# A quarter of the next norm's input, turned by DMA instead of on TensorE

## The chip, the cores and the metric

The kernel runs on one core of one Trainium2 chip. The metric is the device time of one launch in microseconds, as a median over runs.

## The reference

The reference is a two-layer encoder trunk on an input x of 512 tokens by 1024 channels in float32. Each layer adds three branches to x, each behind an RMS norm with a gain per channel, and a last norm ends it:

```python
for l in range(DEPTH):                     # DEPTH = 2
    x = x + 0.5 * swiglu(rms_norm(x, ffn1_norm[l]), ffn1_w_in[l], ffn1_w_out[l])
    x = x + mixer(rms_norm(x, mix_norm[l]), ...)
    x = x + 0.5 * swiglu(rms_norm(x, ffn2_norm[l]), ffn2_w_in[l], ffn2_w_out[l])
return rms_norm(x, final_norm)

def swiglu(x, w_in, w_out):                # w_in 1024 x 5632, w_out 2816 x 1024
    g, u = jnp.split(x @ w_in, 2, axis=-1)
    return (jax.nn.silu(g) * u) @ w_out
```

The mixer joins a neighbourhood attention of eight heads and a two-dimensional Fourier transform per channel group by two gates. Only its beginning matters here: it multiplies its norm's input by a wide matrix, just as an FFN does.

## The kernel before

**Layout and arithmetic.** x lies in SBUF as `x[128, 4, 1024]`: four blocks of 128 tokens, with the tokens on the partitions. A product over channels needs its input the other way round, channels on the partitions, so for each norm x is turned. Every float32 operand of a product is split in two: a high part, rounded by ScalarE (`S.activation(hi, src, AF.Copy)` into float32r), and a low part, the rest, subtracted by VectorE. Three matmuls (high·high, high·low, low·high) make one product. Large products are done by Strassen's scheme with seven products m = 1 to 7 of quarters.

**Weights.** They come in granules of 128 × 1024 (512 KB) in a fixed order, the list of `stage_items`. `Raw.load` asks for one by a DMA on SP's queue. Where the scheme needs the sum of two granules, some sums are made by VectorE (`Item.summed`, L172), others by a second, accumulating DMA from GpSimd's queue (`Raw.summed`, L158), which waits for the first load. `Item.prep` splits a granule (ScalarE L199 or L194, VectorE L202 or L195) into `whi` and `wlo`, which have three buffers each. `Stream.next` hands the next granule to a product after having split up to two more behind it (`AHEAD = 2`); `Stream.prep(to)` splits up to a given place in the list; `fetch` keeps the loads eight granules (`FETCH = 8`) ahead of the splits. `ws` is the stream.

**Order.** Each engine and each queue works in order. The framework lays out the order of every engine when the program is built: instructions that were traced earlier go first, but one whose inputs it believes late is passed by those behind it. Inside `tc.manual_schedule` the engines named keep the written order. `tc.issue_after(ins)` puts instructions of the same engine or queue behind `ins`, without a wait for its end.

**The end of an FFN** (`stage_ffn`, the loop over `steps`). The output product has 21 steps of (m, c), c being one of three chunks of the inner width: (1, 0..2), (2, 0..2), then 5, 6, 7, 3 for each c, and at last (4, 0..2). So steps 6 to 9 are m = 5, 6, 7, 3 with c = 0, steps 14 to 17 the same with c = 2, and 18 to 20 are m = 4. A step with c = 0 has three granule halves (18 matmuls), the others four (24 matmuls). After each step the loop splits inputs of later steps (`make`), and after the last chunk of an m it adds the result to quarters of x (`update`, VectorE, L785). Quarter (i, j) of x is channels half i and token half j; (0,0) has its last update after step 5, the others after steps 14 to 20.

**Turning a quarter** (`Norm.quad_high` and `quad`). Eight TensorE transposes of 128 × 128 (L433) write two PSUM banks `tr`; four activations copy them to `raw` and multiply by the norm's gains (L436); ScalarE rounds the whole to the high part `xh` (L437) and VectorE subtracts the low part `xl` (L438). In the FFN loop quarter (0,0) is turned after step 6, and (1,1) and (0,1) around step 18; (1,0) is left for the next stage. This holds for the first three FFNs; the fourth (`late`) is followed by the final norm, which needs nothing turned.

**Turning by DMA.** The same loop already turns the FFN's inner activations through DMA: `words_apart` (two activations on 16-bit words, L357) separates the two halves of every float32, `turned_words` turns the words by one transposing DMA on SP's queue (L363), and `joined_words` (two activations, L376) puts the halves together again. `released` holds two accumulating loads back until such a turn has landed, by a small DMA into `seen`.

Of the kernel before, what the change touches and what calls it, by code (L numbers as in the profile page):

```python
# [9 lines left out]
F32 = mybir.dt.float32  # L10
# [4 lines left out]
AF = mybir.ActivationFunctionType  # L15
# [5 lines left out]
T = 512  # L21
# [70 lines left out]
def encoder_kernel(  # L92
    ctx: ExitStack, tc: tile.TileContext, xin, xtr, wst, gains, gfin, gbias, bias_in, dft, chan, ident_in, rot, out
):
    nc = tc.nc
    V, S, G, PE = nc.vector, nc.scalar, nc.gpsimd, nc.tensor
# [7 lines left out]
    dp = ctx.enter_context(tc.tile_pool(name="dp", bufs=2, space=bass.MemoryType.DRAM))  # L104
# [3 lines left out]
    def nm(s):  # L108
        uid[0] += 1
        return f"{s}_{uid[0]}"  # L110

    def slot(dt=F32, s="k", shape=(4, 256)):
        return kp.tile([P, *shape], dt, tag="k", name=nm(s), bufs=23)
# [5 lines left out]
    def bank(s="ps"):  # L119
        return pp.tile([P, T], F32, tag="ps", name=nm(s))  # L120
# [5 lines left out]
    x = cp.tile([P, TB, D], F32, tag="x", name="x")  # L126
# [12 lines left out]
    class Raw:  # L139
# [3 lines left out]
        def load(self, parts=1):  # L143
            if self.t is None:
                self.t = raw_pool[0](self.n)
                for c in range(0, self.n, self.n // parts):
                    cs = slice(c, c + self.n // parts)
                    nc.sync.dma_start(out=self.t[:, cs], in_=wst[GRAN_AT[self.key]][:, cs])
                if self.plus:
                    gate = held.get(self.key)  # L150
                    if isinstance(gate, list):
                        gate.append(self)
                    else:
                        with tc.issue_after(gate) if gate else nullcontext():
                            self.summed()
# [48 lines left out]
                G.dma_start(out=t, in_=wst[GRAN_AT[self.then]][:, 0:n], accum_op=ALU.add)  # L204
            self.out = (hi, lo)

    held = {}

    def stage_items():
        items, st = [], 0  # L210
# [72 lines left out]
    class Stream:  # L283
# [32 lines left out]
        def next(self, ahead=AHEAD):  # L316
            self.prep(self.pos + 1 + ahead)
            it = self.items[self.pos]
            self.pos += 1
            return it.out  # L320

    ws = Stream()
# [7 lines left out]
    def split(hi, lo, src, scale=None):  # L330
        if scale is None:
            S.activation(hi, src, AF.Copy)
            V.tensor_tensor(lo, src, hi.bitcast(F32), ALU.subtract)
            return
        S.activation(hi, src, AF.Copy, scale=scale)
        V.scalar_tensor_tensor(lo, src, scale, hi.bitcast(F32), ALU.mult, ALU.subtract)


    def small(s, n=8):
        return sp.tile([P, 8], F32, tag=s, name=nm(s), bufs=2)[:, 0:n]  # L340
# [11 lines left out]
    def words_apart(z):  # L352

        s = slot(U16, "zs", (2, 4, 2, P))
        words = z.bitcast(U16).rearrange("p b (q f h) -> p h q b f", q=4, h=2)
        for h in range(2):
            S.activation(s[:, h], words[:, h], AF.Copy)  # L357
        return s

    def turned_words(s):  # L360

        t = slot(U16, "zt", (2, 4, 256))
        nc.sync.dma_start_transpose(  # L363
            out=t.rearrange("p h q (b t) -> p (h q b) t", b=2), in_=s.rearrange("p h q b f -> p (h q b f)")
        )
        return t

    def apart(z):

        return turned_words(words_apart(z))  # L370

    def joined_words(to, t):

        to = to.bitcast(U16).rearrange("p i (t w) -> p w i t", w=2)
        for w in range(2):
            S.activation(to[:, w], t[:, w], AF.Copy)  # L376

    class Norm:
# [43 lines left out]
        def quad_high(self, i, j):  # L422

            self.tiles(i)
            js = slice(j * 256, (j + 1) * 256)
            hq, lq = self.h[i][:, :, js], self.l[i][:, :, js]
            raw = self.raw[i, j] = slot(F32, "xr")
            for k2 in range(2):
                tr = bank("tr").rearrange("p (a b) -> p a b", a=2)
                for k in range(2):  # L430
                    d = (4 * i + 2 * k2 + k) * P
                    for b in range(2):
                        PE.transpose(tr[:, k, b * P : (b + 1) * P], x[:, 2 * j + b, d : d + P], ident)  # L433
                for k in range(2):
                    kt = 2 * k2 + k
                    S.activation(raw[:, kt, :], tr[:, k, :], AF.Copy, scale=self.gain(4 * i + kt))  # L436
            S.activation(hq, raw, AF.Copy)  # L437
            return lambda: V.tensor_tensor(lq, raw, hq.bitcast(F32), ALU.subtract)  # L438

        def gain(self, kt):  # L440
            c = self.idx * DT + kt
            return gn[:, c : c + 1]
# [185 lines left out]
    def stage_ffn(norm, nxt, late):  # L628
# [25 lines left out]
        raw = norm.raw  # L654
# [247 lines left out]
        for jb in range(0 if first else 1, NB):  # L902
            f0 = 2 + 4 * jb
            if first and jb == 0:
                with tc.manual_schedule(engines={mybir.EngineType.DVE, mybir.EngineType.Activation}):
                    pa = pair("A")
                    product(pa, acts[1], K4, True)
                    for j in range(2):
                        t = snap(pcl[j])
# [39 lines left out]
        if late or nxt.mix:  # L949
            tc.keep_in_program_order(S.activation(small("sq", 1), ones, AF.Sqrt))  # L950
        ps = {}
        for i, (m, c, _) in enumerate(steps):
            make(i)
            if i:
# [25 lines left out]
                    else:  # L980
                        nxt.quad(0, 1)
            make(i + 2)
            if i == 6 and not late:
                nxt.quad(0, 0)
            if m == 4 and c == (0 if late else 1):
                update(ps[1], 1, 0, 1)
            if m == 4 and c == 0 and late:
# [889 lines left out]
    for l in range(L):  # L1877
        nxt = Norm(3 * l + 1)
        stage_ffn(norm, nxt, False)
        norm, nxt = nxt, Norm(3 * l + 2)  # L1880
        stage_mixer(l, norm, nxt)
        norm, nxt = nxt, Norm(3 * l + 3)
# [150 lines left out]
```

## Time and profile before

| what | value |
|---|---|
| median of 3 runs | 1847.23 us (1846.29 to 1848.27) |
| the profiled execution's own time | 1848.74 us |
| its span | 1847.0 us, 1.7 us less than its time |
| granted TensorE clock, mean | 0.998 |
| ScalarE, busy share of the span | 71% |
| GpSimd, busy share of the span | 10% |
| DMA queues of SP and GpSimd, share of 16 engines | 49.9% and 30.1% |
| DMA, mean over the span | 214 GB/s |

The span runs from the first to the last instruction of the profiled execution. A row of a timeline gives the start, the length, the engine, the line of the kernel, the operation with its output and input, and a count, with the idle time before it in brackets. A row of a stretch gives its bounds, its length, and the busy time and instruction count of each engine. PE is TensorE's matmuls, PEld its weight loads, DVE VectorE, ACT ScalarE, POOL GpSimd; SPq is SP's queue of DMA requests.

### The profile page before, as it was taken

How to read it: one execution, taken by the hardware profiler on the slowest of the kernel's cores; microseconds unless marked ns; L12 is line 12 of the kernel's file. 1: busy time of each engine (PE TensorE's matmuls, PEld its weight loads, DVE VectorE, ACT ScalarE, POOL GpSimd, SP SyncE). 2: the span in 40 equal slices, each digit the busy share in tenths (PEclk: the TensorE clock that was granted, in tenths of full speed). 3: DMA queues.
4: the chain of work that ended last, by engine and by line, in shares of the span. 5: the costliest groups of instructions: out<-in, count | busy, mean ns of one | idle time of the engine just before them, and what ended most of it. 6: DMA issues, size and time to landing. Idle time of an engine off the chain costs nothing.

```text
span 1847.0 us, 24568 instructions
## 1 busy us (share of the span) xinstructions
PE 1835.7 (99%) x8850; PEld 1529.2 (83%) x8850; DVE 1602.6 (87%) x1942; ACT 1312.3 (71%) x1777; POOL 175.6 (10%) x215
## 2 busy tenths in 40 slices
PE   9999999999999999999999999999999999999998
PEld 7888888888888888888888888888888888888886
DVE  7878899786989987789998888997869899887898
ACT  6777875668676777787666778766776776777865
POOL 0001011100111010001010100101001101010010
PEclk9999999999999999999999999999999999999999
DMA  9898798933896789879888897989258966888695
GB/s 300 227 231 223 192 271 267 230 118 121 232 234 178 182 207 239 206 208 279 249 194 212 228 221 194 282 283 214 69 182 212 232 173 180 230 218 219 197 278 159
DMA packets 198378, 395.72 MB, mean 214 GB/s; under 512 B 103856, under 2 KB 103984, under 8 KB 198256
## 3 DMA queue, kind: packets, MB, share of 16 engines
q1 hardware_dynamic: 168912, 294.23, 49.9%
q0 software_dynamic: 28912, 99.38, 30.1%
q8 instruction: 69, 1.13, 0.2%
q10 hardware_dynamic: 432, 0.55, 0.1%
q14 instruction: 53, 0.43, 0.1%
HBM read 367.88 MB, written 2.11 MB: 200 GB/s over the span
## 4 chain that ended last, share of the span: by engine, by line
PE 94%; DVE 3%; issue 1%; DMA 1%; ACT 0%; POOL 0%; SPq 0%; DVEq 0%; ACTq 0%; POOLq 0%
PE A L521 10%; PE A L524 10%; PE A L522 10%; PE o L524 6%; PE o L521 6%; PE o L522 6%; PE B L521 5%; PE B L522 5%; PE B L524 5%; PE ps L326 4%; PE ps L327 3%; PE ps L328 3%; PE C L521 3%; PE C L522 3%; PE C L524 3%
## 5 line engine op out<-in xcount | busy, mean ns | idle before, releaser
L202 DVE TENSOR_TENSOR wlo<-raw,whi 128x1024 fp32r<-128x1024 f32 (+1 forms) x532 | 630.9, 1196 | 174.4 <-ACT whi L199 173.5
L199 ACT ACTIVATE whi<-raw 128x1024 fp32r<-128x1024 f32 (+1 forms) x532 | 544.0, 1033 | 263.4 <-PE A L522 53.6
L158 POOL DMA_DIRECT2D raw<-in_wst_dram x166 | 145.1, 898 | 1283.1 <-DMA raw<-in_wst_dram 530.5
L172 DVE TENSOR_TENSOR raw<-raw,raw 128x1024 f32<-128x1024 f32 (+1 forms) x148 | 177.0, 1196 | 2.0
L522 PE MATMUL A<-whi,xl 128*128 128x512 f32 x400 | 155.7, 389 | 0.0
L521 PE MATMUL A<-whi,xh 128*128 128x512 f32 x400 | 155.7, 389 | 0.0
L376 ACT ACTIVATE at<-zt 128x1024 uint16<-128x1024 uint16 (+2 forms) x96 | 110.3, 1166 | 15.1 <-DMA zt<-zs 15.0
L194 ACT ACTIVATE whi<-raw 128x1024 fp32r<-128x1024 f32 (+1 forms) x83 | 85.3, 1034 | 45.8 <-issue 12.5
L524 PE MATMUL A<-wlo,xh 128*128 128x512 f32 x400 | 115.0, 389 | 0.0
L195 DVE SCALAR_TENSOR_TENSOR wlo<-raw,whi 128x1024 fp32r<-128x1024 f32 (+1 forms) x83 | 98.6, 1198 | 13.1 <-ACT whi L194 13.1
L524 PEld LDWEIGHTS A<-wlo,xh 128*128 128x128 f32 x400 | 75.1, 188 | 15.5
L522 PEld LDWEIGHTS A<-whi,xl 128*128 128x128 f32 x400 | 75.1, 188 | 15.4
L521 PEld LDWEIGHTS A<-whi,xh 128*128 128x128 f32 x400 | 75.1, 188 | 15.4
L521 PE MATMUL C<-whi,xh 128*128 128x512 f32 x208 | 81.1, 390 | 0.2 <-ACT whi L199 0.2
L522 PE MATMUL C<-whi,xl 128*128 128x512 f32 x208 | 81.0, 389 | 0.0
L522 PE MATMUL B<-whi,xl 128*128 128x512 f32 x208 | 81.0, 389 | 0.0
L521 PE MATMUL B<-whi,xh 128*128 128x512 f32 x208 | 80.9, 389 | 0.0
L357 ACT ACTIVATE zs<-th 128x1024 uint16<-128x1024 uint16 x80 | 79.5, 1042 | 1.0 <-DVE th L766 0.9
L759 ACT ACTIVATE th<-sn,rh 128x512 f32<-128x512 f32 x80 | 55.1, 716 | 35.0 <-DVE sn L596 34.2
L591 ACT ACTIVATE sn<-A 128x512 f32<-128x512 f32 x104 | 59.2, 585 | 24.2 <-PE A L524 24.2
L524 PE MATMUL C<-wlo,xh 128*128 128x512 f32 x208 | 59.8, 389 | 0.0
L524 PE MATMUL B<-wlo,xh 128*128 128x512 f32 x208 | 59.8, 389 | 0.0
(429 smaller groups left out, 4686.6 us busy)
## 6 DMA issues: line engine op xcount, KB each, us to landing
raw<-in_wst_dram SPq DMA_DIRECT2D x468, 512.0 KB, 6.1
raw<-in_wst_dram POOLq DMA_DIRECT2D x176, 512.0 KB, 8.0
bm<-in_bias_dram SPq DMA_DIRECT2D x16, 512.0 KB, 4.1
raw<-in_wst_dram SPq DMA_DIRECT2D x30, 256.0 KB, 4.5
x<-in_xin_dram SPq DMA_DIRECT2D x4, 512.0 KB, 10.2
raw<-in_wst_dram POOLq DMA_DIRECT2D x8, 256.0 KB, 8.2
dft<-in_dft_dram POOLq DMA_DIRECT2D x8, 256.0 KB, 10.6
gb<-in_gbias_dram SPq DMA_DIRECT2D x4, 512.0 KB, 9.2
```

The lines of the kernel that those rows point to most:

```text
L158: G.dma_start(out=self.t, in_=wst[GRAN_AT[self.plus]][:, 0 : self.n], accum_op=ALU.add)
L172: V.tensor_tensor(self.raw.t, self.raw.t, self.add.t, ALU.add)
L194: S.activation(hi, t, AF.Copy, scale=-1.0)
L195: self.last = V.scalar_tensor_tensor(lo, t, -1.0, hi.bitcast(F32), ALU.mult, ALU.subtract)
L199: S.activation(hi[:, cs], t[:, cs], AF.Copy)
L202: self.last = V.tensor_tensor(lo[:, cs], t[:, cs], hi[:, cs].bitcast(F32), ALU.subtract)
L326: PE.matmul(ps, lh, rh, start=start, stop=False, skip_group_check=again)
L357: S.activation(s[:, h], words[:, h], AF.Copy)
L376: S.activation(to[:, w], t[:, w], AF.Copy)
L521: PE.matmul(ps, lh, rh, start=start, stop=False, skip_group_check=again)
L522: PE.matmul(ps, ll, rh, start=False, stop=False, skip_group_check=again)
L524: PE.matmul(ps, lh, rl, start=False, stop=stop, skip_group_check=again)
```

## The change

At the ends of the first three FFNs, quarter (0,0) of the next norm's input is no longer turned on TensorE after step 6. A generator, `turned_quad`, does it in four parts. After step 13 ScalarE takes the words of the quarter apart. After step 14 the words are turned by one DMA on SP's queue. This DMA stands behind a small read (16 floats to DRAM, into `seen`) of the granule whose accumulating sum was asked for last (`newest_sum`), so that SP's queue holds until that sum has landed. After step 16 ScalarE joins the words. After step 17 come the four scalings by the gains, now from SBUF to SBUF in place, and the split into high and low part. Just ahead of that last part `ws.prep(ws.pos + 3)` asks for the split of one more granule of weights. Only quarter (0,0) is moved.

```diff
@@ Raw.load @@
                 if self.plus:
+                    newest_sum[0] = self
                     gate = held.get(self.key)
...
-    held = {}
+    held, newest_sum = {}, [None]
...
+    def behind(raw):
+
+        seen = dp.tile([16], F32, tag="seen", name=nm("seen"))
+        to = bass.AP(tensor=seen.tensor, offset=seen.offset, ap=[[16, 1], [1, 16]])
+        return tc.issue_after(nc.sync.dma_start(out=to, in_=raw.t[0:1, 0:16]).ins)
...
+        def turned_quad(self, i, j):
+
+            js = slice(j * 256, (j + 1) * 256)
+            s = words_apart(x[:, 2 * j : 2 * j + 2, i * T : (i + 1) * T])
+            yield
+            with behind(newest_sum[0]):
+                t = turned_words(s)
+            yield
+            self.tiles(i)
+            raw = self.raw[i, j] = slot(F32, "xr")
+            joined_words(raw, t)
+            yield
+            for k in range(4):
+                S.activation(raw[:, k, :], raw[:, k, :], AF.Copy, scale=self.gain(4 * i + k))
+            split(self.h[i][:, :, js], self.l[i][:, :, js], raw)
+            yield
@@ stage_ffn, the loop over steps @@
         ps = {}
+        quad00 = nxt.turned_quad(0, 0)
         for i, (m, c, _) in enumerate(steps):
...
             make(i + 2)
-            if i == 6 and not late:
-                nxt.quad(0, 0)
+            if i == 17 and not late:
+                ws.prep(ws.pos + 3)
+            if i in (13, 14, 16, 17) and not late:
+                next(quad00)
             if m == 4 and c == (0 if late else 1):
```

## The prediction

> **What bounds the kernel now.** I read the page first, then the waits of TensorE, then busy time by stretch at the places that the change touches, and last the single instructions there.
>
> ```profile
> PE 1835.7 (99%) x8850; PEld 1529.2 (83%) x8850; DVE 1602.6 (87%) x1942; ACT 1312.3 (71%) x1777; POOL 175.6 (10%) x215
> PE 94%; DVE 3%; issue 1%; DMA 1%; ACT 0%; POOL 0%; SPq 0%; DVEq 0%; ACTq 0%; POOLq 0%
> ```
> ```profile
> PE ps L136 <- DVE ones L132: 1.2, 1, 1.2
> PE cl L522 <- DVE xl L336: 0.3, 1, 0.3
> PE o L524 <- DVE wlo L202: 0.2, 1, 0.2
> ```
>
> TensorE is busy for 99% of the span, holds 94% of the chain that ended last, and its longest listed wait is 1.2 us, at the start. So an instruction taken from TensorE is worth its own time, as long as nothing behind it becomes late; and there is next to no waiting left that a better order could win back. VectorE, at 87% on average, is the engine to watch.
>
> The change touches three places, the ends of the first three FFNs. I number the output products of an FFN as the loop does, 0 to 20. The eight transposes of quarter (0,0) run between products 6 and 7, and the fourth FFN runs the same two products without them:
>
> ```profile
> 254.20 1.03 PE L433 MATMUL tr<-ident,x 128*128 128x128 f32 x8
> 254.99 0.49 PE L521 MATMUL o<-whi,c6h 128*128 128x512 f32 x1
> ```
> ```profile
> 250.11:259.21 9.10, 9.10 (x45) 7.58 (x44) 9.10 (x12) 7.97 (x15) 1.73 (x2) 1.00 0.98 222
> 847.23:856.33 9.10, 9.10 (x45) 7.58 (x44) 9.10 (x12) 7.70 (x15) 1.73 (x2) 1.00 0.92 211
> 1166.30:1175.40 9.10, 9.10 (x46) 7.58 (x44) 9.10 (x12) 7.98 (x15) 1.73 (x2) 1.00 1.04 253
> 1762.31:1770.47 8.16, 8.16 (x37) 6.76 (x36) 8.16 (x11) 6.36 (x10) 0.00 (x0) 1.00 1.03 263
> ```
>
> After length and busy time of TensorE come weight loads, VectorE, ScalarE, GpSimd, the granted clock (1.00), the DMA share and GB/s. The two products take 9.10 us with the transposes and 8.16 us without.
>
> **Part 1, taken away: eight transposes at each of three ends.** 9.10 − 8.16 = 0.94 us each, more than the 0.79 us from the first transpose to the next product, since the matmuls right behind them are slower too. Three times 0.94 is 2.82 us.
>
> **Part 2, added on ScalarE and moved on VectorE.** Prices of one instruction:
>
> ```profile
> 255.18 1.55 ACT L436 ACTIVATE xr<-tr,gn 128x256 f32<-128x256 f32 x4
> 259.54 1.23 DVE L438 TENSOR_TENSOR xl<-xr,xh 128x1024 fp32r<-128x1024 f32 x1
> ```
> ```profile
> L376 ACT ACTIVATE mq<-zt x8: 1348/1359/1367, 527.2 to 1455.8; 128x1024 uint16<-128x1024 uint16 x8
> L363 SPq DMA_TRANSPOSE zt<-zs x44: 1317/3365/5361, 72.5 to 1738.9; - x44
> L357 ACT ACTIVATE zs<-fs x8: 1049/1050/1057, 517.8 to 1439.8; 128x1024 uint16<-128x1024 uint16 x8
> DMA to landing us min/median/max: 4.3/5.5/7.4
> ```
>
> ScalarE takes the words apart (2 × 1.05 us) and joins them (2 × 1.36 us): 4.8 us more at each end. The four scalings stay four, now reading SBUF; the trace has none of that form, so I take the 1.55 us of the four that read PSUM (bounds: half of it and twice it, 0.8 to 3.1 us; either end stays inside the idle time shown below). The rounding to the high part and VectorE's 1.23 us for the low part stay, but move from products 6 and 7 to products 17 and 18. The room for it:
>
> ```profile
> 283.69:305.45 21.76, 21.76 (x97) 18.02 (x96) 21.76 (x23) 10.70 (x11) 1.73 (x2) 1.00 0.82 245
> 880.81:902.57 21.76, 21.76 (x97) 18.02 (x96) 21.76 (x23) 11.61 (x12) 1.73 (x2) 1.00 0.82 249
> 1199.88:1221.64 21.76, 21.76 (x98) 18.02 (x96) 21.76 (x23) 10.74 (x12) 1.73 (x2) 1.00 0.83 257
> 305.45:311.60 6.15, 5.94 (x25) 4.35 (x24) 6.15 (x7) 4.85 (x9) 0.55 (x1) 1.00 0.95 372
> 902.57:908.01 5.44, 5.44 (x25) 4.51 (x24) 5.44 (x8) 4.23 (x9) 0.00 (x0) 1.00 0.88 281
> 1221.64:1227.08 5.44, 5.44 (x26) 4.51 (x24) 5.44 (x7) 4.77 (x8) 0.56 (x1) 1.00 1.00 401
> ```
>
> The first three rows are products 13 to 16, the last three product 17. ScalarE is idle for 10 to 11 of 21.76 us, so 4.8 us find cover there; if that cover were gone, ScalarE's roundings of weights, which VectorE and then TensorE wait for, would be late by as much. VectorE is busy for the whole of every row: it has no slack of its own, only the lead that it holds over TensorE. At the first end that lead is used up already: product 17 takes 6.15 us where the other two ends take 5.44, 0.71 us lost.
>
> What this does to the gain hangs on whether VectorE moves forward with TensorE. It loses the 1.23 us early. At the second and third end it is busy throughout, so it comes that much earlier and the lead is kept: gain 0.94 us each. At the first end it stands at a transfer in between:
>
> ```profile
> 277.83 2.01 ACT L199 ACTIVATE whi<-raw 128x1024 fp32r<-128x1024 f32 x2 [1.75 <-DMA raw<-in_wst_dram]
> ```
> ```profile
> 278.93 1.22 DVE L202 TENSOR_TENSOR wlo<-raw,whi 128x1024 fp32r<-128x1024 f32 x1 [1.06 <-ACT whi L199]
> ```
>
> ScalarE waits 1.75 us for weights and VectorE 1.06 us for ScalarE; if that transfer lands when it did, the 1.23 us run into this wait, and TensorE, 0.94 us earlier, meets a VectorE that is no earlier. I count nothing won at the first end (bounds: 0.94 + 0.71 = 1.65 won if the transfer also comes sooner; 0.8 lost by the next step).
>
> **Part 3, the low part ahead of the updates of x.** In program order the split now stands before the last updates of x at product 17, and quarter (0,1)'s transposes, the second eight in the next rows of TensorE, read what these write:
>
> ```profile
> 313.57 2.49 DVE L785 SCALAR_TENSOR_TENSOR x<-o,x 128x512 f32<-128x512 f32 x4
> ```
> ```profile
> 315.70 1.91 PE L433 MATMUL tr<-ident,x 128*128 128x128 f32 x16
> ```
> ```profile
> 1228.58 2.51 DVE L785 SCALAR_TENSOR_TENSOR x<-o,x 128x512 f32<-128x512 f32 x4
> ```
> ```profile
> 1231.16 1.91 PE L433 MATMUL tr<-ident,x 128*128 128x128 f32 x16
> ```
>
> The updates end at 316.06 and 1231.09, the second eight begin 0.79 us after the row's start, at 316.49 and 1231.95: 0.43 and 0.86 us to spare. With as much VectorE work before them as ever and TensorE 0.94 us earlier, the third end pays 0.1 us. The first, if its early relief is lost, pays 1.23 − 0.43 = 0.8 us against before. The granule asked for one place sooner stands ahead of the split, so its own parts aren't late; it adds no work, I cost it at nothing, and without it the 1.23 us would stand ahead of a low part that product 19 needs.
>
> **Part 4, the turn on SP's queue.** The small read waits in SP's queue until the newest sum has landed; behind it wait the transpose and every later load. The sums and their landing at the three ends:
>
> ```profile
> 288.48 0.86 POOL L158 DMA_DIRECT2D raw<-in_wst_dram  x1 [0.35 <-DVE wlo L202]
> ```
> ```profile
> 297.66 1.06 ACT L199 ACTIVATE whi<-raw 128x1024 fp32r<-128x1024 f32 x1 [0.80 <-DMA raw<-in_wst_dram]
> 301.96 1.06 ACT L199 ACTIVATE whi<-raw 128x1024 fp32r<-128x1024 f32 x1 [3.24 <-DVE raw L172]
> 302.93 0.83 ACT L332 ACTIVATE c4h<-at 128x768 fp32r<-128x768 f32 x1
> 306.57 2.01 ACT L199 ACTIVATE whi<-raw 128x1024 fp32r<-128x1024 f32 x2 [2.81 <-DVE raw L172]
> ```
> ```profile
> raw<-in_wst_dram SPq DMA_DIRECT2D x468, 512.0 KB, 6.1
> ```
> ```profile
> 294.57:300.01 5.44, 5.44 (x25) 4.51 (x24) 5.44 (x8) 3.35 (x4) 0.00 (x0) 1.00 0.56 178
> 891.69:897.13 5.44, 5.44 (x25) 4.51 (x24) 5.44 (x8) 1.92 (x2) 0.00 (x0) 1.00 0.31 109
> 1210.76:1216.20 5.44, 5.44 (x26) 4.51 (x24) 5.44 (x8) 2.19 (x3) 0.00 (x0) 1.00 0.44 147
> ```
>
> At the first end the last sum leaves at 288.48 and ScalarE has it at 297.66. The turn follows, 5.5 us to landing (4.3 to 7.4): about 303.2. The three stretches below the load's row are product 15 at the three ends. It falls there or just behind, where the DMA share is only 0.31 to 0.56, so it delays little. Loads behind it lose some 4 us (3.4 us of SP's queue and the read); they are asked for eight granules ahead, some 22 us (a product of two granules takes 5.44 us), against 6.1 us to landing: nothing reaches TensorE. The joining needs 2.6 to 2.7 us, and ScalarE has 2.81 us free just then, from 303.76 to 306.57. That fits, with nothing over: with the slowest landing, 7.4 us, the joining ends 1.2 us late. I cost the median case at nothing.
>
> By the Trainium skill, "Advanced Engine Details and Errata", section "X-Bar Transpose (TRN2)", a transpose by DMA is as fast as a plain one, 350 to 400 GB/s; for the turn's 512 KB that is an estimate of 1.3 to 1.5 us, and by it the wait for the turn would drop out. The row's 5.5 us differ, and I go by the row.
>
> **Sum.** −2.82 (part 1) + 0.94 (nothing won at the first end) + 0.1 (third end) = −1.8 us. On the profiled execution that is 1848.74 to 1846.9; from the median, 1847.23 to 1845.4. Bounds: −2.82 − 0.71 = −3.5, so 1843.7; upwards the rivals. About 0.2%, 3.7 us, is what a measurement of this kernel can tell from no change: the whole of part 1 lies within it.
>
> **Rivals.** *VectorE eats it all.* All three ends become bound by VectorE, and the first pays the 0.8 us of part 3: 0 to +0.8, about 1847.5. For it: VectorE full in every row. Against: the lead holds at two ends. Chance 0.18.
>
> *ScalarE stands at the joining.* Its order is fixed when the program is built; if the joining is put ahead of a rounding of weights and the turn lands late, the rounding, VectorE and TensorE are late together, for the gap of 2.81 us is already filled by the copies. Price: the longest wait for a turn before is
>
> ```profile
> ACT at L376 <- DMA zt<-zs: 15.0, 7, 3.0
> ```
>
> 3.0 us; at all three ends 9.0 − 2.82 = +6.2, 1853.4. It decides "slower" from (2.82 + 3.7)/3 = 2.2 us an end. For it: two transfers in series now stand before the turn's result. Against: two products, 10.9 us, lie between asking and joining. Chance 0.19. The Trainium skill, "VectorE: DVE Perf Modes", section "Rules for kernel authors", would have a 128×128 transpose on TensorE when PSUM will do; the trace agrees on latency (0.79 us against 5.5 us), and this rival is where that latency would count.
>
> *A better order.* The rebuilt order also frees the 0.71 us and a little elsewhere: below 1843.5, chance 0.07. TensorE's waits leave hardly more. The forecast, 1843.6 to 1846.5, has the remaining 0.56.
>
> **How the numbers follow.** Faster by over 0.2% 0.07; within 0.56 + 0.18 = 0.74; slower 0.19. The range, 1843.6 to 1851.5, takes in the forecast, the first rival and the milder half of the second; some 0.16 lies outside.
>
> **What would show it.** Right: products 6 and 7 take 8.16 us at all ends; L433 has 24 transposes fewer; product 17 of the first end is no shorter than 6.15 us, and a wait for x stands before quarter (0,1)'s transposes there. Wrong: ScalarE's wait for the turned words over 2 us an end; SP's loads late at the next stage; products 17 to 19 longer at the second end, where I see slack.

## The result, and the profile after

The change makes the kernel slower: 1853.94 us (median of 7 runs, 1851.41 to 1858.27) against 1848.21 us of the kernel before in the same session (7 runs, 1846.29 to 1850.57). The ratio is 1.0033, with an interval of 1.0023 to 1.0043. The profiled execution took 1855.46 us, its span 1853.7 us. The prediction said 1845.4 us and at most 1851.5.

From the page of the changed kernel: TensorE's line of busy time, and the shares of the chain that ended last. Below them the waits of TensorE, from its view of waits.

```profile
PE 1837.0 (99%) x8826; PEld 1525.5 (82%) x8826; DVE 1603.0 (86%) x1942; ACT 1324.1 (71%) x1789; POOL 175.6 (9%) x215
PE 86%; DMA 5%; DVE 4%; issue 2%; ACT 1%; SPq 0%; POOL 0%; DVEq 0%; ACTq 0%; POOLq 0%
```
```profile
PE tr L440 <- DVE x L809: 3.5, 4, 1.6
PE ps L136 <- DVE ones L132: 1.2, 1, 1.2
PE o L545 <- ACT whi L200: 1.1, 2, 0.6
PE o L548 <- DVE wlo L203: 0.8, 2, 0.7
```

TensorE has 24 instructions fewer and is still 99% busy, but it holds only 86% of the chain that ended last, where it had 94%, and DMA has risen from 1% to 5%. There is a wait for x that was not there before, ahead of the transposes of the other quarters (L440), and waits for weights.

Where the time went is best read in stretches of the output product. Three views of stretches follow; the three rows of each group are the ends of the first, second and third FFN. First the changed kernel: products 6 and 7, products 10 to 13, and products 14 to 20.

```profile
250.12:258.28 8.16, 8.16 (x38) 6.76 (x36) 8.16 (x11) 6.36 (x10) 1.73 (x2) 1.00 0.99 241
847.16:855.32 8.16, 8.16 (x38) 6.76 (x37) 8.16 (x11) 5.35 (x9) 1.73 (x2) 1.00 0.96 218
1169.90:1178.06 8.16, 8.16 (x37) 6.76 (x36) 8.16 (x11) 6.36 (x10) 1.73 (x2) 1.00 0.95 234
266.44:288.20 21.76, 21.76 (x98) 18.02 (x96) 20.80 (x20) 12.43 (x13) 3.95 (x5) 1.00 1.05 319
863.48:886.38 22.90, 22.34 (x97) 17.87 (x96) 18.55 (x17) 11.83 (x13) 4.32 (x5) 1.00 1.03 298
1186.22:1207.98 21.76, 21.76 (x97) 18.02 (x96) 19.23 (x18) 11.36 (x12) 4.44 (x6) 1.00 1.03 309
```
```profile
288.20:328.26 40.06, 39.36 (x179) 31.89 (x178) 38.24 (x41) 30.14 (x45) 2.63 (x4) 1.00 0.94 279
886.38:928.39 42.01, 39.73 (x180) 31.82 (x178) 41.20 (x45) 31.90 (x46) 3.45 (x4) 1.00 0.89 246
1207.98:1249.69 41.71, 40.28 (x179) 31.66 (x178) 39.89 (x43) 31.05 (x46) 3.02 (x4) 1.00 0.90 275
```

Then products 10 to 13 and 14 to 20 of the kernel before, which the prediction does not show in this cut:

```profile
267.37:289.13 21.76, 21.76 (x97) 18.02 (x96) 20.70 (x19) 12.11 (x13) 4.49 (x6) 1.00 1.04 304
864.49:886.25 21.76, 21.76 (x97) 18.02 (x96) 21.76 (x20) 12.39 (x13) 3.45 (x4) 1.00 1.04 302
1183.56:1205.32 21.76, 21.76 (x98) 18.02 (x96) 21.76 (x21) 12.23 (x13) 3.94 (x5) 1.00 1.03 300
```
```profile
289.13:328.39 39.26, 39.05 (x180) 31.95 (x178) 37.22 (x41) 24.65 (x36) 2.48 (x4) 1.00 0.84 259
886.25:924.79 38.54, 38.54 (x180) 32.12 (x179) 38.16 (x42) 26.93 (x39) 2.59 (x3) 1.00 0.81 227
1205.32:1243.85 38.53, 38.53 (x179) 32.12 (x178) 36.06 (x40) 24.69 (x36) 2.27 (x3) 1.00 0.85 260
```

Products 6 and 7 give 0.94 us at each end, as forecast: −2.82. Products 10 to 13 lose 1.14 at the second end. Products 14 to 20 lose 0.80, 3.47 and 3.18. Together +5.8 us; of the 6.7 us between the two spans the other 0.9 lie in the fourth FFN, which the change does not touch.

The third busy time of a row is VectorE's. In products 10 to 13 it was full at the second and third end before; after, it is idle for 4.35 us of 22.90 and 2.53 us of 21.76. At the first end it is idle for about 1 us before and after. With that idle time the loss begins. The timeline of ScalarE and of VectorE in the changed kernel's second end shows what it stands at:

```profile
872.98 1.06 ACT L200 ACTIVATE whi<-raw 128x1024 fp32r<-128x1024 f32 x1 [4.21 <-DMA raw<-in_wst_dram]
876.63 2.01 ACT L200 ACTIVATE whi<-raw 128x1024 fp32r<-128x1024 f32 x2 [2.58 <-DMA raw<-in_wst_dram]
```
```profile
874.08 1.23 DVE L203 TENSOR_TENSOR wlo<-raw,whi 128x1024 fp32r<-128x1024 f32 x1 [3.08 <-PE o L546]
877.72 1.23 DVE L203 TENSOR_TENSOR wlo<-raw,whi 128x1024 fp32r<-128x1024 f32 x1 [1.28 <-ACT whi L200]
```

ScalarE waits 4.21 and 2.58 us for weights, and VectorE stands behind it (the first of its waits is put down to TensorE, but it begins again within 0.05 us of the end of that rounding). These are the two weights of product 12, each summed by a second, accumulating transfer from GpSimd's queue; the view of these two transfers names ScalarE's rounding as what waited for them, 4.2 and 2.6 us. The timeline of GpSimd, the same two sums, first before and then after:

```profile
861.27 0.87 POOL L158 DMA_DIRECT2D raw<-in_wst_dram  x1 [10.05 <-DMA raw<-in_wst_dram]
862.53 0.86 POOL L158 DMA_DIRECT2D raw<-in_wst_dram  x1 [0.39 <-issue]
```
```profile
863.86 0.87 POOL L159 DMA_DIRECT2D raw<-in_wst_dram  x1 [11.61 <-DMA raw<-in_wst_dram]
865.08 0.86 POOL L159 DMA_DIRECT2D raw<-in_wst_dram  x1 [0.36 <-issue]
```

Product 10 began at 864.49 before and at 863.48 after. So the sums left 3.2 and 2.0 us ahead of it, and now leave 0.4 and 1.6 us behind its start. They also take longer to land, 9.0 and 11.4 us where they took 7.6 and 10.2. Before, they landed 1.7 and 0.1 us ahead of ScalarE's roundings (870.58 and 872.81): there was next to no margin. Each sum waits for the load that it adds to. The load under the second was asked for no later than before (853.93 against 854.28), but landed after 10.6 us instead of 7.7; the DMA share around it, 853 to 862, is 0.98 here and was 1.03.

Late weights make VectorE late, and then its order at product 17 counts. VectorE's and TensorE's timelines in the changed kernel, second end (L809 updates x, L334 is the split of c4 or of the quarter, L440 the other quarters' transposes):

```profile
909.57 0.68 DVE L809 SCALAR_TENSOR_TENSOR x<-o,x 128x512 f32<-128x512 f32 x1
...
912.27 0.68 DVE L809 SCALAR_TENSOR_TENSOR x<-o,x 128x512 f32<-128x512 f32 x1
912.87 1.23 DVE L203 TENSOR_TENSOR wlo<-raw,whi 128x1024 fp32r<-128x1024 f32 x1
914.01 0.68 DVE L809 SCALAR_TENSOR_TENSOR x<-o,x 128x512 f32<-128x512 f32 x1
914.76 1.23 DVE L334 TENSOR_TENSOR xl<-xr,xh 128x1024 fp32r<-128x1024 f32 x1
915.90 0.68 DVE L809 SCALAR_TENSOR_TENSOR x<-o,x 128x512 f32<-128x512 f32 x1
```
```profile
914.75 0.33 PE L440 MATMUL tr<-ident,x 128*128 128x128 f32 x1 [0.65 <-DVE x L809]
916.64 0.98 PE L440 MATMUL tr<-ident,x 128*128 128x128 f32 x7 [1.56 <-DVE x L809]
```

The extra granule's low part and the moved quarter's stand between the last four updates of x, and TensorE's transposes wait 0.65 and 1.56 us for these.

### The profile page after: what moved, and what is told of

The parts are those of the page before. It is cut to its first block, busy times and chain, and to the rows that moved or that the text cites. A ratio compares the mean times of both kernels' runs of the same rounds, so it can differ in the third digit from the quotient of the medians.

```text
span 1853.7 us, 24539 instructions
## 1 busy us (share of the span) xinstructions
PE 1837.0 (99%) x8826; PEld 1525.5 (82%) x8826; DVE 1603.0 (86%) x1942; ACT 1324.1 (71%) x1789; POOL 175.6 (9%) x215
## 4 chain that ended last, share of the span: by engine, by line
PE 86%; DMA 5%; DVE 4%; issue 2%; ACT 1%; SPq 0%; POOL 0%; DVEq 0%; ACTq 0%; POOLq 0%
PE A L545 10%; PE A L548 10%; PE A L546 10%; PE B L545 5%; PE B L546 5%; PE B L548 5%; DMA raw<-in_wst_dram 5%; PE o L545 4%; PE o L546 4%; PE o L548 4%; PE ps L327 4%; PE ps L328 3%; PE ps L329 3%; PE C L545 2%; PE C L546 2%; PE C L548 2%
## 6 DMA issues: line engine op xcount, KB each, us to landing
x<-in_xin_dram SPq DMA_DIRECT2D x4, 512.0 KB, 10.2
```

## The experiments

All times are medians in us. A trace shows one execution of a kernel, which need not be near its median; where it is not, the text says so. The kernel before had 1848.2 (1847.9 to 1848.9 by session, 7 to 33 runs). Each ratio is to the kernel before in its own session, with its 95% interval.

| kernel | median (range), runs | ratio |
|---|---|---|
| the change | 1853.94 (1851.41–1858.27), 7 | 1.0033 [1.0023, 1.0043] |
| 1 updates of x first | 1849.97 (1846.71–1855.28), 11 | 1.0008 [0.9999, 1.0017] |
| 2 no extra granule | 1853.2 (1852.15–1857.97), 6 | 1.0032 [1.0019, 1.0044] |
| 3 turn not held | 1851.61 (1847.89–1853.26), 11 | 1.0017 [1.0008, 1.0026] |
| 4 updates first, not held | 1851.21 (1849.28–1855.0), 11 | 1.0016 [1.0007, 1.0025] |
| 5 before, transposes left out | 1849.98 (1846.03–1852.32), 11 | 1.0010 [1.0001, 1.0019] |
| 6 before, transposes done twice | 1851.42 (1849.02–1854.49), 11 | 1.0017 [1.0008, 1.0026] |
| 7 before, quarter moved only | 1851.08 (1847.9–1854.36), 11 | 1.0014 [1.0005, 1.0023] |
| 8 before, fewer sums | 1845.75 (1845.22–1846.93), 11 | 0.9989 [0.998, 0.9998] |
| 9 no transposes, fewer sums | 1844.88 (1844.34–1845.83), 11 | 0.9982 [0.9973, 0.9991] |
| 10 change, fewer sums | 1844.29 (1843.47–1845.03), 8 | 0.9976 [0.9966, 0.9986] |
| 11 updates first, fewer sums | 1844.81 (1844.16–1846.9), 11 | 0.9981 [0.9972, 0.999] |
| 12 moved only, fewer sums | 1847.66 (1847.07–1848.9), 11 | 0.9996 [0.9987, 1.0005] |
| 13 before, sums aside | 1847.6 (1846.03–1848.7), 11 | 0.9996 [0.9987, 1.0005] |
| 14 change, sums aside | 1845.98 (1843.73–1848.66), 11 | 0.9987 [0.9979, 0.9996] |
| 15 change, GpSimd adds | 1864.14 (1863.09–1865.18), 4 | 1.0083 [1.007, 1.0097] |
| 16 before, GpSimd adds | 1864.73 (1861.39–1865.44), 5 | 1.0085 [1.0071, 1.0099] |
| 17 change, GpSimd adds at two chunks | 1878.64 (1878.19–1881.46), 4 | 1.0165 [1.0151, 1.0179] |
| 18 change, VectorE adds | 1857.99 (1856.16–1859.11), 5 | 1.0051 [1.0037, 1.0064] |

The first theory was A: the loss is the wait for x. The rivals then put it on the extra granule, on the hold of SP's queue, or on the removed transposes being worth nothing.

**1. Updates of x first.** The extra granule and the last part of the turned quarter stand behind the updates and squares.

```diff
-            if i == 17 and not late:
-                ws.prep(ws.pos + 3)
-            if i in (13, 14, 16, 17) and not late:
+            if i in (13, 14, 16) and not late:
                 next(quad00)
...
                 update(ps[3], 0, 1, 1)
                 nxt.squares(0, 1)
+                if not late:
+                    ws.prep(ws.pos + 3)
+                    next(quad00)
```

> The changed kernel with one edit: the granule asked for ahead, the four scalings and the split come behind the updates of x of product 17 instead of ahead of them. Theory A (the loss has two parts: some 4.9 us at products 18 to 20 because the updates of x come late on VectorE and TensorE waits for x before quarter (0,1)'s transposes, and some 2 to 3 us at products 11 to 17 because weight sums land no sooner and VectorE runs dry): 4 to 5 us less than the changed kernel, about 1849, within 1 us of the kernel before; TensorE's wait for x goes from 3.5 us to under 1 us. Rival B (SP's queue, held by the small read, delays the loads behind it): no change, 1854. Rival C (ScalarE's 4.6 us more per end delay the roundings): no change, 1854.

About 4 us came back, and the wait for x is gone from TensorE's waits. What remains at their head is another one:

```profile
PE o L548 <- DVE wlo L203: 2.3, 5, 0.7
```

So by the medians the order does cost what A says, but with x in time the kernel is still no faster than before: the 2.8 us are missing. The trace is of one of the two slowest executions of this kernel, 1853.89, and shows no more than that the wait is gone: its products 14 to 20 still take 41.14, 38.53 and 41.76 us at the three ends, against 39.26, 38.54 and 38.53 before.

**2. No extra granule.**

```diff
-            if i == 17 and not late:
-                ws.prep(ws.pos + 3)
```

> The changed kernel without the granule that is asked for ahead of the scalings and the split; the split still stands ahead of the updates in program order. Theory A in the form that the granule's low part, 1.2 us on VectorE, is what stands between the updates of x: as good as the kernel with the updates first, about 1849, and TensorE's wait for x under 1 us. If it is the quarter's own split that delays them: half of that at most, 1851.5 to 1854. Rivals B and C: no change, 1854.

Nothing is gained. The wait for x goes, and a larger one takes its place, for the rounding of product 19's weights, which now stands behind the joining and the scalings:

```profile
PE o L545 <- ACT whi L200: 3.2, 2, 1.6
```

The extra granule is needed where the quarter's split is; it is not by itself the cause.

**3. The turn not held behind the newest sum**, and **4.** the same with the updates first.

```diff
-            with behind(newest_sum[0]):
-                t = turned_words(s)
+            t = turned_words(s)
```

> The changed kernel without the small read: the turn is issued as soon as the words are apart, SP's queue is not held until the newest sum has landed. Rival B: the loads behind it come up to 9 us sooner and most of the loss goes, 1848 to 1850. Theory A: no gain, 1853 to 1855, or a little slower since the turn then runs beside the accumulating loads.

> The change with two of its edits altered together: the extra granule and the quarter's split stand behind the last updates of x and its squares, and the transpose by DMA is not held behind the newest weight load (no small read). Each alone gave about 2 to 4 us back from the change's 1854: 1850.0 for the first, 1851.6 for the second. Theory A (the updates' place, and apart from it the hold, which delays weights at products 10 to 12 or SP's queue): the two add up in part, 1847.5 to 1849, which is at the kernel before's 1848.2 or just under. Rival (without the hold only the order at product 17 changed for the better, which the first edit does as well): 1850, as with the first edit alone.

Alone it took 2.3 us off, more than A allows, though its interval touches that of the change. With the updates first it gave nothing: 1851.21 against 1849.97. So the hold has no cost of its own that these runs can show.

**5. The transposes left out of the kernel before**, nothing moved. (The scalings read x unturned.)

```diff
             if i == 6 and not late:
-                nxt.quad(0, 0)
+                nxt.unturned(0, 0)
```

> The kernel before with one part left out: the eight transposes of quarter (0,0) at the three ends; the four scaling copies at the same place read x as it lies, so the quarter is not turned at all, and nothing is added elsewhere. It prices the removed TensorE time alone. The prediction's part 1 with the lead kept at all ends: 2.8 us less than before, about 1845. Theory A with VectorE and the weight sums as the bound behind it: 0 to 1.5 us less, 1846.5 to 1848, with new idle time of VectorE behind ScalarE and the weights between products 9 and 12 at all three ends.

This is the change's whole gain alone, and it came out at +1.8 us instead of −2.8. Products 10 to 13 again, at the three ends:

```profile
266.04:287.88 21.84, 21.84 (x98) 17.94 (x96) 19.29 (x18) 11.00 (x12) 4.33 (x5) 1.00 1.04 312
864.01:885.77 21.76, 21.76 (x98) 18.02 (x96) 19.36 (x18) 11.71 (x12) 4.35 (x6) 1.00 1.03 309
1183.33:1205.50 22.17, 22.17 (x97) 17.86 (x96) 19.28 (x18) 11.01 (x12) 4.89 (x6) 1.00 1.05 321
```

VectorE is now idle for 2.4 to 2.9 us at every end, with no turn by DMA, no moved split and no extra granule in the kernel. TensorE pays behind that: products 14 to 17 take 23.75, 22.95 and 23.76 us, where they took 22.47, 21.76 and 21.76. So TensorE's gain is lost before anything that the change adds comes in. One rival is left here: the framework lays out the order anew, and at these ends VectorE's order differs from the kernel before in some 30 places and ScalarE's in some 20. Run 9 settles it.

**6. The transposes done twice**, the opposite.

```diff
-                nxt.quad(0, 0)
+                nxt.quad(0, 0, 2)
```

> The kernel before with each of the eight transposes of quarter (0,0) done twice, at the same place: 24 transposes more, some 2.4 to 2.8 us of TensorE. If an instruction on TensorE is worth its own time there, 1850.5 to 1851. If TensorE's time at that place is taken up by what VectorE and the weights allow (which is why leaving them out gained nothing), 1847.5 to 1849.

```profile
PE 1838.1 (99%) x8874; PEld 1531.8 (83%) x8874; DVE 1602.5 (87%) x1942; ACT 1312.6 (71%) x1777; POOL 175.8 (10%) x215
```

Twenty-four more instructions cost 3.1 us, slightly over their own time (products 6 and 7 take 9.98, 9.97 and 9.97 us, 0.87 more at each end). TensorE's time at this place costs in full when added, and with the sums in place it is worth nothing when removed. The reading is that TensorE and the supply of split weights reach these products at about the same moment.

**7. The quarter moved, still turned on TensorE**, behind the updates, with the extra granule.

```diff
-            if i == 6 and not late:
-                nxt.quad(0, 0)
...
                 nxt.squares(0, 1)
+                if not late:
+                    ws.prep(ws.pos + 3)
+                    nxt.quad(0, 0)
```

> The kernel before with quarter (0,0) moved as a whole: its eight transposes, scalings and split stand at product 17 behind the last updates of x, with the extra granule ahead of them; nothing is turned by DMA. TensorE does what it did. Theory M (the move is what costs: VectorE's 1.23 us and ScalarE's roundings crowd products 17 to 20): 1850 to 1852, no better than the change with the updates first (1850). Rival T (the DMA turn with its 4.8 us of ScalarE per end costs): within 1 us of the kernel before, 1847.5 to 1849.

The move alone costs 2.9 us, the amount that theory M gave, so the turn by DMA is not needed for a loss. The place that M named does not bear it out: in the trace (1851.26) products 6 to 20 take 233.6 us at the three ends together, against 233.9 before. What is lost stands ahead of the fourth FFN's output product, 1.8 us between 1243.9 and 1734.0, and in its products 10 to 13, 0.9 us, where the orders of VectorE and ScalarE are those of the kernel before. One trace can't tell whether the move does this or that execution.

**8 to 12. Fewer sums.** If late summed weights are the cause, the same comparisons without those sums must come out as forecast. The four accumulating transfers of the middle chunk (c = 1), in each FFN's output product, are left out:

```diff
-                r[q] = [Raw(key(q, g), n, q2 and key(q2, g)) for g, n in enumerate(sizes)]
+                q3 = None if (name(q)[0], idx) == ("o", 1) else q2
+                r[q] = [Raw(key(q, g), n, q3 and key(q3, g)) for g, n in enumerate(sizes)]
```

> The kernel before without the four summing transfers of the middle chunk's weights in every FFN's output product (2.1 MB per FFN less; those weights are not summed), transposes kept. The control for the run without transposes. Since the kernel before hardly waits for weights anywhere (0.71 us at product 17 of the first end, about 2 us in the fourth FFN's middle products by the run), 1845 to 1848 by either theory.

> The kernel before without the eight transposes at three ends (the scalings read x unturned), and also without the four summing transfers of the middle chunk's weights in every FFN's output product (four of 512 KB in products 6 to 13, 2.1 MB per FFN; the sums are left out, so those weights are not summed). To be read against the same cut in the kernel with the transposes. Theory S (the transposes alone gained nothing since the weights of products 10 to 12 land no sooner, so VectorE and ScalarE wait there): with the cut those loads come earlier, and leaving the transposes out is now worth 2 to 2.8 us against the kernel with transposes and the same cut. Rival O (VectorE's order at products 17 to 20, which the planner makes anew, takes the gain): the difference stays within 0.7 us either way.

> The change as it is, without the four summing transfers of the middle chunk's weights in every FFN's output product (2.1 MB per FFN; those weights are not summed). With the same cut the kernel before takes 1845.75 us, and without the transposes 1844.9. Theory A+S (two causes that add: TensorE's waits for x behind the granule and the split, some 4 us, which more room for weights doesn't mend; and the supply of weights, which takes the gain of the transposes): 1847 to 1849, with waits of TensorE for x still there. Rival (all of it is the supply of weights: with the cut the change gains what it was meant to): 1843.5 to 1845.

> The change with the extra granule and the quarter's split behind the last updates of x, and without the four summing transfers of the middle chunk's weights in every FFN's output product (those weights are not summed). Theory A+S (with x in time and room for weights the transposes' time is won as in the run without them): 1844.3 to 1845.3, under the kernel before with the same cut (1845.75) by 0.5 to 1.5 us. Rival M (the moved VectorE work costs by itself at products 17 to 20, about 3 us as in the move without DMA turn): 1847 to 1849.

> The kernel before with quarter (0,0) moved to product 17 behind the updates, transposes kept, and without the four summing transfers of the middle chunk's weights in every FFN's output product (those weights are not summed). If the 3.0 us that the move cost came by way of the weights' supply, 1845.5 to 1846.5, as the kernel before with that cut (1845.75); if it is VectorE's and ScalarE's order at products 17 to 20, 1848 to 1849.

The order of instructions on VectorE, ScalarE and SP's queue is the same, one for one, as with the sums, for the kernel before and for the change. Yet the change, 5.7 us slower with the sums, is now 1.46 us faster than its control (1844.29 against 1845.75; by the means of the runs −1.6, with an interval of −2.1 to −1.0; the two were measured in different sessions). Putting the updates first adds nothing (1844.81).

Leaving the transposes out is worth 0.9 us (interval 0.5 to 1.4) of the whole, neither the 2 to 2.8 of theory S nor the 0.7 at most of rival O. The trace of run 9 shows the rest. Products 6 and 7 take 8.16 us at all three ends, and this is products 10 to 20:

```profile
266.21:326.67 60.46, 60.46 (x276) 50.28 (x275) 58.39 (x60) 35.94 (x46) 5.72 (x7) 1.00 0.90 279
861.75:922.21 60.46, 60.46 (x276) 50.30 (x275) 59.70 (x61) 39.38 (x51) 6.04 (x7) 1.00 0.84 240
1179.88:1240.34 60.46, 60.46 (x276) 50.29 (x275) 58.39 (x60) 35.94 (x46) 5.76 (x7) 1.00 0.90 277
```

The control takes 60.45, 60.46 and 60.46 us. So at the three ends the whole 2.8 us are won, and the order of VectorE, ScalarE and TensorE in run 9 is that of run 5, one for one: the new order is not what cost run 5 its gain. Some 1.7 us are lost again elsewhere, in the two stretches from the first and the third end to the next output product, 488.84 and 489.35 us against 488.18 and 488.28 in the control.

Products 10 to 13 of the change without these sums:

```profile
266.33:288.09 21.76, 21.76 (x97) 18.02 (x96) 21.76 (x21) 13.51 (x14) 3.46 (x4) 1.00 0.91 261
862.25:884.01 21.76, 21.76 (x98) 18.02 (x97) 21.76 (x20) 13.40 (x14) 3.46 (x4) 1.00 0.92 258
1180.46:1202.22 21.76, 21.76 (x97) 18.02 (x96) 21.76 (x21) 13.51 (x14) 3.48 (x4) 1.00 0.91 265
```

VectorE is full at all three ends, and TensorE waits for x nowhere. So theory A+S, two causes that add, was wrong in its first half: the order at product 17 costs 4 us only with the sums in place, when VectorE arrives late. The runs also draw together: they spread over 1.6 us with the change where they spread over 6.9. The move alone still loses here, by 1.9 us, but not at the three ends: in its trace (1848.87, near its slowest) products 6 to 20 take 233.15 us there together, just as in the control.

**13 and 14. The sums turned aside.** What of a sum costs: the time in which it holds the DMA engines, or the chain from load to sum to rounding? At the same places of GpSimd's queue the loaded weights are now added into a buffer in HBM that nobody reads.

```diff
+                if self.aside:
+                    G.dma_start(out=asides[0][:, 0 : self.n], in_=self.t, accum_op=ALU.add)
+                    asides.append(asides.pop(0))
```

> The kernel before with the same four transfers turned aside into a buffer in HBM (those weights are not summed). The control: Theory R 1848 to 1849, as the kernel before; Theory L 1845.5 to 1846.5, as without these transfers (1845.75).

> The change with the four summing transfers of the middle chunk turned aside: at the same places of GpSimd's queue, each of the four loaded weights is added by DMA, 512 KB, into a buffer in HBM that nobody reads (so those weights are not summed). Theory R (the DMA engines' time): the loads are as late as in the change, 1851 to 1855. Theory L (the chain from load to sum to rounding): the roundings no longer wait for a second transfer, 1844 to 1846, as without these transfers (1844.3).

The change stays ahead of its control, by 1.6 us (by the means −1.4, interval −2.5 to −0.4), and lies where theory L had it (1844 to 1846). The control, 1847.6, lies between the two theories: over the 1846.5 of L, under the 1848 of R. Products 10 to 13 of the change, from a trace of its slowest execution (1848.66):

```profile
266.41:288.17 21.76, 21.76 (x97) 18.02 (x96) 21.76 (x21) 13.50 (x14) 4.39 (x6) 1.00 1.05 318
861.99:883.75 21.76, 21.76 (x97) 18.02 (x96) 21.76 (x20) 13.39 (x14) 3.47 (x4) 1.00 1.05 309
1180.19:1201.95 21.76, 21.76 (x97) 18.02 (x96) 20.86 (x20) 10.05 (x10) 3.48 (x4) 1.00 1.04 300
```

The DMA engines are as loaded as in the change (1.04 to 1.05, last but one column), and VectorE is full at two ends and idle for 0.9 us at the third. The engines' time costs both kernels about the same, 1.85 us before (1847.6 − 1845.75) and 1.7 after (1845.98 − 1844.29). The need for the sum costs the kernel before another 0.3 to 0.6 us and the change 8: this is the difference between the two. For the change theory L holds. That execution still loses 3.0 us in products 14 to 20 of its third end, so the cure is not complete in every execution.

**15 to 18. Another way to sum.** Two of the four sums are c + a for product 7, and a is in SBUF already. GpSimd, or VectorE, can add it; nothing is left out.

```diff
+                elif here:
+                    add(c, a, on=G)
                 else:
                     add(c)
```

> The change, and in the middle chunk of every FFN's output product the two weights of product 7 (c + a) are summed by GpSimd from the a that lies in SBUF for product 6, instead of by a summing transfer; nothing is left out (1.0 MB less by DMA per FFN). Theory R (room in the DMA engines decides): half of the transfers of the earlier cut are gone, so part of the way from 1854 to the cut's 1844.3: 1845 to 1849, TensorE's waits for x gone or shorter. Rival G (the cut helped by what it left out, or GpSimd's add takes long or gets in VectorE's way): 1852 or more.

> The kernel before with the same: in the middle chunk GpSimd adds a to c in SBUF for product 7, in place of two summing transfers per FFN. The control. Theory R: 1846 to 1847.5, between the kernel before (1848.2) and the one with four transfers less (1845.75), so at or above the change with the same. Rival G: 1848 to 1850.

> The change with GpSimd's adds in the middle and the last chunk of every FFN's output product (four summing transfers less per FFN, 2.1 MB, nothing left out). Theory R: 1844 to 1847, the change's gain all there, and below the kernel before by 1 to 4 us. Rival G: GpSimd's adds, if each is several us long, make product 7's weights late: 1850 or more, with TensorE waiting for the weights of the products 7.

> The change, and in the middle chunk the two weights of product 7 are summed by VectorE from the a that lies in SBUF, in place of two summing transfers (nothing left out). VectorE gets 2 x 1.14 = 2.3 us more at each of four ends and has no slack at products 13 to 17. If its waits for weights at products 10 to 12 (2.5 to 4.4 us at the second and third end) go away with the two transfers, they pay for this: 1848 to 1851, better than the change. If not, 2.3 us times four on top: 1860 to 1864.

The rival G won with GpSimd; the kernel before with its adds missed both ranges, 1864.73 against 1850 at most. From the groups of GpSimd and of VectorE in run 15, by line and shape:

```profile
L174 POOL TENSOR_TENSOR raw<-raw,raw 128x1024 f32<-128x1024 f32 x8 | 50.8, 6368 | 32.4 <-DMA raw<-in_wst_dram 19.4 <-DVE wlo L204 9.6 <-DVE at L810 3.4
```
```profile
L174 DVE TENSOR_TENSOR raw<-raw,raw 128x1024 f32<-128x1024 f32 x140 | 170.5, 1219 | 2.0
```

One add takes 6.37 us on GpSimd and 1.22 us on VectorE. Two in a row also hold GpSimd's queue, with the other sums in it, for 13 us, so these runs say nothing on the DMA engines. On VectorE the kernel takes 4 us more than the change, 1857.99, in the gap between the two ranges expected. The Trainium skill, "GPSIMD Engine Reference", in its opening part, puts VectorE at roughly twice GpSimd's speed in elementwise arithmetic; here it was 5.2 times, and the measurement decides. GpSimd's adds ran beside a VectorE that was busy for 85 to 95% of products 10 to 13; how much of the difference that makes was not tried. No version that computes the reference came out faster than the kernel before; the best form of the change is number 1, at 1.0008.

## Why the prediction was wrong

**Part 1, the transposes.** Their size was right to the hundredth: 8.16 us for products 6 and 7 at all three ends, 24 instructions fewer. The prediction's own condition, that an instruction taken from TensorE is worth its own time as long as nothing behind it becomes late, was not met, and it was not looked up where it counts. The transposes left out alone gave +1.8 us; in that trace the first two ends came out 0.4 and 0.2 us longer than before and the third 1.5 us, where 0.94 us a piece were to be won.

**Part 2, VectorE's lead.** This is the step that failed. The prediction took "busy throughout" at the second and third end as "it comes that much earlier", and saw a late weight only at the first end, where the row of 1.75 us stood in the trace. But VectorE was full at the other ends because summed weights came just in time, 1.7 and 0.1 us ahead of their roundings at the second; with TensorE 0.94 us earlier they were needed before they were there. VectorE's own relief of 1.23 us is not what it takes: run 5 keeps that work where it was and has the same idle time. The trace before shows the lack of margin to a reader who asks for the time from a sum's issue to its use, and at the third end a row of the same kind as the one of 1.75 us stood in it:

```profile
1192.64 1.06 ACT L199 ACTIVATE whi<-raw 128x1024 fp32r<-128x1024 f32 x1 [1.19 <-DMA raw<-in_wst_dram]
```

What came in place of the 0.94 us won at each of these two ends was a loss of 3.7 us net at the second and 2.2 us at the third. ScalarE's 4.8 us for taking apart and joining did find room, and the quarter's words were never waited for. With the four sums gone, products 14 to 20 of the change take 38.98, 38.62 and 38.98 us where the control takes 38.53, 38.53 and 38.54: −2.82 + 0.98 = −1.8 us (measured −1.46 in the medians). That this is the prediction's sum is luck in part: it was to come from two ends won whole and one not at all, and came from three, each won and in part lost again.

**Part 3, the low part ahead of the updates.** The mechanism was right, the size wrong. Waits for x stand ahead of the transposes, 3.5 us in all, where the sum has 0.1 and a bound 0.8 more: the margins of 0.43 and 0.86 us were those of a VectorE that is in time, and the second end, where none was counted, has the longest. That products 17 to 19 of the second end would be longer is one of the prediction's own signs of being wrong. Product 17 of the first end, in turn, took 5.84 us, less than the 6.15 that it gave as a sign of being right. The extra granule, costed at nothing, adds no work, but at the second end its 1.14 us slipped between the updates; without it product 19's weights are late (run 2).

**Part 4, SP's queue.** The turn was there in time at all three ends; no wait for its words stands in the trace. Its rows at the second, from the view of the turned words' tile:

```profile
L383 ACT ACTIVATE xr<-zt x2: 1355/1356/1357, 904.9 to 906.1; 128x1024 uint16<-128x1024 uint16 x2
L364 SPq DMA_TRANSPOSE zt<-zs x1: 2928/2928/2928, 895.3 to 895.3; - x1
DMA to landing us min/median/max: 4.8/4.8/4.8
```

Asked for at 895.3, landed 4.8 us later, joined at 904.9. The Trainium skill's figure for the transpose ("Advanced Engine Details and Errata", "X-Bar Transpose (TRN2)") again gives too little here: 4.8 and 5.9 us at the two ends where the landing is on record, against an estimate of 1.3 to 1.5. The hold of the queue showed no cost of its own (run 4).

**The rivals.** The result, 1853.9, lies by chance next to the price of "ScalarE stands at the joining", 1853.4; that rival is refuted, for ScalarE waited for no turned word. "VectorE eats it all" named the right engine and stopped at 0 to +0.8, since it let VectorE be as early as before and no earlier weights be needed. No rival had weights as the next bound. The range ended at 1851.5, 2.4 us short.

**What stays open.** Why the loss is larger than the lead lost: the changed kernel's waits for weights are 4.21 and 2.58 us where VectorE was only some 1.2 us earlier. The trace shows loads that were asked for no later but landed later, with the DMA engines as full as before; which transfers went ahead of them, no run tested. Nor is it settled why the moved quarter alone costs 1.9 us even with fewer sums (run 12), and why run 9 keeps 0.9 us of its 2.8: neither is lost at the three ends.

## What to carry to other kernels

Here an engine that was 99% busy, with another at 100% behind it, was not one bound but two that arrived together: adding work cost in full, and removing it gave nothing. So it may be elsewhere. Before an instruction on TensorE is costed at its own time, follow each stretch behind it to the transfer that feeds it, and compare the time from issue to landing with the time to use; a sum made by two transfers in series needs margin for both. An order that is harmless while an engine is in time can cost several microseconds once it is late, so a move and its margin have to be priced with the engine late as well.

## What the runs showed of the hardware

An elementwise add of 128 × 1024 float32 took 6.37 us on GpSimd, beside a busy VectorE, against 1.22 us on VectorE. Four accumulating transfers of 512 KB per FFN, turned to HBM where nobody read their result, cost 1.7 to 1.9 us of the whole. The spread of the runs goes with such sums: the kernel before spread over 3 to 7 us, by session, and the change and runs 1 to 7 over 5 to 9 us, and without the sixteen sums of the middle chunks the kernels spread over less than 2 us in four of five cases (2.7 in the fifth). Turned aside, the same transfers leave a spread of 2.7 us before and 4.9 with the change.
